# Modulated norms with plain transposes: the shift leaves the matmul and is added per feature tile when PSUM is emptied

## The chip, the cores and the metric

The kernel runs on one core of a Trainium2 chip, in one launch. The metric is the device time of one execution in microseconds (us), taken as the median of several executions; one execution of the kernel before was also recorded by the hardware profiler. Engines are named as in the profile: PE is the matrix engine (PEld its weight loads), DVE the vector engine, ACT the scalar engine, POOL the GpSimd engine, SP the engine that issues most of the DMAs. A name such as L598 is a line of the kernel.

## The reference

A stack of transformer blocks on 256 tokens of width 1024, batch 1, all in f32. The first two blocks use plain RMS norms; the last two ("mix2" and "ffn2", two layers each) are conditioned on a vector c: per layer a product of silu(c) with a matrix (1024 x 6144) gives six vectors of 1024, a shift, a scale and a gate for each half of the block.

```python
y = x * rsqrt(mean(x * x, axis=-1) + 1e-6)
h = y * (n * (1 + scale)) + shift      # per feature, before mix2 and before ffn2
x = x + gate * mix2(h)                 # three mixers side by side, one output product
x = x + gate * ffn2(h)                 # causal depthwise conv on a gated feed-forward
```

What matters here is the second line: a norm whose result has a per-feature shift added, and which must reach the products with features on the 128 partitions.

## The kernel before

The 256 tokens are two token tiles of 128 (t = 0, 1), the 1024 features eight feature tiles of 128 (k = 0 to 7). x is kept with tokens on partitions. Every large product is done in three passes: each operand is split into a rounded high part and the low remainder (h_hi and h_lo for activations, wh and wl for weights), and hi*hi, lo*hi and hi*lo are accumulated in PSUM. A weight tile is brought by a DMA on SP's queue into raw, rounded to wh by ACT (CAST, L464), and its remainder wl is made by POOL (L467) or DVE (L469).

The program runs eight stages one after the other; the last four are m0 (mix2, layer 0, from about 787 us), f2 (ffn2, layer 0, from 967), m1 (mix2, layer 1, from 1184) and f3 (ffn2, layer 1, from 1367, to the end at 1569). Each of the four begins with a norm with shift, and these four norms are all that the change touches. The other norms have no shift.

A norm (`_norm`, L582) works per token tile and per half of the features. DVE multiplies x by the inverse root and by `row`, a copy of n * (1 + scale) on all partitions (L595), which gives xn. A PSUM tile ps_t of 128 x 512 then takes four 128 x 128 blocks. Without a shift each is a PE transpose (L605). With a shift a first matmul (L598) writes the shift into all of ps_t: its operand is the last 128 columns of the tile `row`, which are zero (a POOL memset, L557) but for eight rows that hold the shift (a DMA, L558), and the other operand is the identity, broadcast. The four blocks are then added by ordinary matmuls with the identity (L603), into the same accumulation. Emptying is the same for both: one ACT copy of 128 x 512 rounds ps_t to h_hi (L608), one DVE subtraction of 128 x 512 makes h_lo (L609).

Who reads h: in m0 and m1 `rwkv_scores` computes ps_lk (eight feature tiles of three matmuls for t0, then the same for t1; L492, L493, L494 of `mm3_b`) and copies each result out (a_raw, L1527), and the other mixers follow on the same h. In f2 and f3 `first_units` (L612) computes ps_gt in the same way for each token tile, copies it (first_raw, L627) and transposes it (L634); all further units use ps_gu (L480, L483).

The conditioning vectors come from 24 products on DVE per layer (`ada_step`, L1394), each on a 1 MB piece that ACT's queue brings (L1378); those of layer 1 run during f2. `mod_rows` packs the results, transposes them on PE and writes them to DRAM, from where `load_row` (L551) fetches the rows back. The shift is in the 48-column tile mods[l] with features on partitions as well, columns 0 to 7 for the mixer and 24 to 31 for the feed-forward.

The order of the instructions on each engine is not written by hand: the kernel's framework schedules every engine's queue from the program order, priorities and its own time estimates. Each engine then runs its queue strictly in that order, so an instruction that waits holds up all that is behind it.

## Time and profile before

| | |
|---|---|
| median of 3 runs | 1570.32 us (1565.72 to 1572.02) |
| the profiled execution | 1570.74 us, span in the trace 1569.0 us |
| mean granted PE clock | 0.972 of full speed |
| PE busy | 1455.1 us (93% of the span) |
| PE weight loads | 1286.3 us (82%) |
| DVE busy | 1120.2 us (71%) |
| ACT busy | 811.7 us (52%) |
| POOL busy | 659.3 us (42%) |

How to read it: the share of an engine is an average over eight stages that have different limits, so the rows further down come from single stages. A timeline row gives the start, the time until the end of the group, the engine, the line, the operation with the tiles that it writes and reads, the count, and in brackets how long the engine had been idle and what released it. PE's matmuls overlap, so the distance between two starts tells what one costs, not its duration.

### The profile page before, as it was taken

The numbers are of one execution on the slowest core, as the hardware profiler recorded it, in microseconds if no ns is written. First come the engines' busy times: TensorE is split into PE (matmuls) and PEld (weight loads), VectorE is DVE, ScalarE is ACT, GpSimd is POOL, SyncE is SP. The second block draws the span as 40 slices with busy tenths as digits, with TensorE's granted clock in tenths as the row PEclk, the third lists the DMA queues.
The fourth block names the chain that finished last, engine by engine and source line by source line (L and its number), as shares of the span: only waits on it lengthen the run. The fifth ranks groups of instructions, "written<-read, shape, count | busy, mean of one in ns | idle before, by whom it ended". The sixth has DMA issues, their size and how long they took to land. (4 is left out here: it accounts for less than half of the span.)

```text
span 1569.0 us, 25783 instructions
## 1 busy us (share of the span) xinstructions
PE 1455.1 (93%) x9586; PEld 1286.3 (82%) x9586; DVE 1120.2 (71%) x2352; ACT 811.7 (52%) x1474; POOL 659.3 (42%) x433
## 2 busy tenths in 40 slices
PE   5999989899999899999988988998998899899998
PEld 4998878699988788999877766898987776589987
DVE  3588668778686577887477597788876768766752
ACT  4676545544543464554354665455544465466651
POOL 3577623256452522443136312465644622236530
PEclk9999999999999999999998999999999999999999
DMA  4756622677884455988434325576773442465551
GB/s 159 232 167 189 182 69 68 209 289 281 298 306 131 136 182 188 337 313 311 170 115 128 108 78 184 203 285 252 264 247 126 120 130 72 141 202 180 191 188 38
DMA packets 103246, 292.96 MB, mean 187 GB/s; under 512 B 28072, under 2 KB 37968, under 8 KB 96976
## 3 DMA queue, kind: packets, MB, share of 16 engines
q1 hardware_dynamic: 93872, 237.12, 44.9%
q10 hardware_dynamic: 8896, 53.14, 9.2%
q8 instruction: 75, 1.23, 0.3%
q0 software_dynamic: 352, 1.06, 0.2%
q14 instruction: 51, 0.42, 0.1%
HBM read 288.04 MB, written 3.24 MB: 186 GB/s over the span
## 5 line engine op out<-in xcount | busy, mean ns | idle before, releaser
L467 POOL TENSOR_TENSOR wl<-raw,wh 128x1024 fp32r<-128x1024 f32 (+4 forms) x162 | 405.6, 2511 | 414.6 <-ACT wh L464 350.7
L464 ACT CAST wh<-raw 128x1024 fp32r<-128x1024 f32 (+3 forms) x421 | 424.1, 1018 | 249.1 <-PE ps_o L493 97.4
L469 DVE TENSOR_TENSOR wl<-raw,wh 128x1024 fp32r<-128x1024 f32 (+2 forms) x259 | 356.9, 1385 | 145.2 <-ACT wh L464 143.2
L480 PE MATMUL ps_gu<-h_hi,wh 128*128 128x256 f32 x1280 | 313.1, 283 | 6.9 <-DVE gu_u L2226 6.3
L480 PE MATMUL ps_gu<-h_lo,wh 128*128 128x256 f32 x1280 | 312.7, 283 | 0.0
L480 PEld LDWEIGHTS ps_gu<-h_hi,wh 128*128 128x128 f32 x1280 | 244.9, 191 | 7.6 <-issue 6.7
L480 PEld LDWEIGHTS ps_gu<-h_lo,wh 128*128 128x128 f32 x1280 | 245.0, 191 | 0.1
L1394 DVE CUSTOM_DVE_ANT_0 ada_raw<-ada_raw,ada_cond 128x1024 f32<-128x1024 f32 x96 | 160.5, 1685 | 68.7 <-DMA ada_raw<-in_ada 68.7
L483 PE MATMUL ps_gu<-h_hi,wl 128*128 128x256 f32 x1280 | 179.2, 283 | 5.9 <-DVE wl L469 3.9
L483 PEld LDWEIGHTS ps_gu<-h_hi,wl 128*128 128x128 f32 x1280 | 164.4, 192 | 6.5 <-DVE wl L469 4.1
L494 PE MATMUL ps_o<-wl,act_h 128*128 128x512 f32 x352 | 138.8, 394 | 0.0
L493 PE MATMUL ps_o<-wh,act_l 128*128 128x512 f32 x352 | 138.6, 394 | 0.0
L492 PE MATMUL ps_o<-wh,act_h 128*128 128x512 f32 x352 | 138.3, 393 | 0.0
L2226 DVE SCALAR_TENSOR_TENSOR gu_u<-ps_gu,f2s,gu_u 128x254 f32<-128x254 f32 (+1 forms) x176 | 82.0, 477 | 40.7 <-ACT gu_u L2224 38.6
L738 POOL TENSOR_TENSOR act_l<-gu_t,act_h 128x256 fp32r<-128x256 f32 x44 | 51.8, 1179 | 102.7 <-ACT act_h L737 102.7
L2229 POOL TENSOR_TENSOR gu_t<-gu_t,gu_u 128x256 f32<-128x256 f32 x44 | 47.4, 1078 | 97.4 <-DVE gu_u L2226 84.1
L494 PEld LDWEIGHTS ps_o<-wl,act_h 128*128 128x128 f32 x352 | 66.1, 188 | 15.4 <-issue 0.5
L493 PEld LDWEIGHTS ps_o<-wh,act_l 128*128 128x128 f32 x352 | 66.1, 188 | 15.1 <-issue 0.2
L492 PEld LDWEIGHTS ps_o<-wh,act_h 128*128 128x128 f32 x352 | 66.1, 188 | 15.0 <-issue 0.2
L737 ACT CAST act_h<-gu_t 128x256 fp32r<-128x256 f32 x44 | 17.7, 407 | 95.8 <-DVE gu_t L736 95.8
L480 PE MATMUL ps_g<-h_hi,wh 128*128 128x256 f32 x256 | 66.5, 294 | 0.0
L480 PE MATMUL ps_g<-h_lo,wh 128*128 128x256 f32 x256 | 66.2, 293 | 0.0
(662 smaller groups left out, 2978.1 us busy)
## 6 DMA issues: line engine op xcount, KB each, us to landing
ada_raw<-in_ada ACTq DMA_DIRECT2D x48, 1024.0 KB, 6.2
raw<-in_f_gu SPq DMA_DIRECT2D x88, 512.0 KB, 5.4
raw<-in_u_gu SPq DMA_DIRECT2D x88, 512.0 KB, 4.2
raw<-in_f_dn SPq DMA_DIRECT2D x44, 512.0 KB, 6.2
raw<-in_u_dn SPq DMA_DIRECT2D x44, 512.0 KB, 4.3
raw<-in_g_qkv SPq DMA_DIRECT2D x32, 512.0 KB, 3.5
raw<-in_g_z SPq DMA_DIRECT2D x16, 512.0 KB, 5.7
raw<-in_g_out SPq DMA_DIRECT2D x16, 512.0 KB, 3.7
```

Of the source, the lines that this page charges most:

```text
L464: self.last_copy = nc.scalar.copy(wh[:, :cols], raw[:, :cols])
L467: nc.gpsimd.tensor_tensor(wl[:, :cols], raw[:, :cols], wh[:, :cols].bitcast(F32), op=ALU.subtract)
L469: nc.vector.tensor_tensor(wl[:, :cols], raw[:, :cols], wh[:, :cols].bitcast(F32), op=ALU.subtract)
L480: nc.tensor.matmul(ps, wh[:, k * width + m0 : k * width + m0 + m], xx[:, k, :], start=(n == 0), stop=(n == last))
L483: self.last_mm = nc.tensor.matmul(ps, wl[:, k * width + m0 : k * width + m0 + m], xh[:, k, :], start=False, stop=(n == last))
L492: nc.tensor.matmul(ps, xh, wh[:, sl], start=start, stop=False, **kw)
L493: nc.tensor.matmul(ps, xl, wh[:, sl], start=False, stop=False, **kw)
L494: nc.tensor.matmul(ps, xh, wl[:, sl], start=False, stop=stop, **kw)
L738: nc.gpsimd.tensor_tensor(al[:, m, :], t, ah[:, m, :].bitcast(F32), op=ALU.subtract)
L1394: nc.vector.tensor_tensor_reduce(raw[:, j], raw[:, j], self.cond, 1.0, 0.0, op0=ALU.mult, op1=ALU.add, accum_out=mod[:, i : i + 1])
L2226: nc.vector.scalar_tensor_tensor(u[:, j, d:], ps[:, j, : S - d], cw[:, 3 * q + 2 - d : 3 * q + 3 - d], u[:, j, d:], op0=ALU.mult, op1=ALU.add)
L2229: nc.gpsimd.tensor_tensor(t, t, u[:, 0], op=ALU.mult)
```

## The change

The shift matmul, the 128 extra columns of `row`, their memset and the DMA of the shift are gone. Norms with a shift now use the plain transposes. Emptying is per feature tile: ACT's activation (Identity, with the shift as a bias column) makes one 128 x 128 block of h_hi, and one DVE instruction, (ps_t + shift) - h_hi, makes the block of h_lo. `mod_rows` packs four vectors rather than six, which drops two small DVE copies per layer. `norm_steps` gets the columns of mods[l] in place of True.

```diff
-    def load_row(self, src, shift=None, queue=None):
-        self.row = self.xp.tile([128, D + 128], F32, name="row", tag="row")
-        queue = queue or self.nc.sync
-        queue.dma_start(self.row[:, :D], src.partition_broadcast(128))
-        if shift is not None:
-            self.nc.gpsimd.memset(self.row[:, D:], 0.0)
-            queue.dma_start(self.row[0:8, D:], shift)
+    def load_row(self, src, queue=None):
+        self.row = self.xp.tile([128, D], F32, name="row", tag="row")
+        (queue or self.nc.sync).dma_start(self.row, src.partition_broadcast(128))
...
                         ps = self.pm.tile([128, 4, 128], F32, name="ps_t", tag="mm")
-                        if shift:
-                            nc.tensor.matmul(ps, self.row[:, D:], self.ident[:, 4 * i : 4 * i + 4].unsqueeze(2).to_broadcast([128, 4, 128]), start=True, stop=False, skip_group_check=True)
                         for j in range(4):
                             k = i * 4 + j
-                            xk = xn[:, k * 128 : k * 128 + 128]
-                            if shift:
-                                nc.tensor.matmul(ps[:, j, :], xk, self.ident, start=False, stop=j == 3, skip_group_check=True)
-                            else:
-                                nc.tensor.transpose(ps[:, j, :], xk, self.ident)
+                            nc.tensor.transpose(ps[:, j, :], xn[:, k * 128 : k * 128 + 128], self.ident)
                         tk = slice(t * 128, t * 128 + 128)
+                        if shift is not None:
+                            for j in range(4):
+                                k = i * 4 + j
+                                nc.scalar.activation(h[:, k, tk], ps[:, j], AF.Identity, bias=shift[:, k : k + 1], scale=1.0)
+                                nc.vector.scalar_tensor_tensor(l[:, k, tk], ps[:, j], shift[:, k : k + 1], h[:, k, tk].bitcast(F32), op0=ALU.add, op1=ALU.subtract)
+                            continue
                         hs, ls = (a[:, 4 * i : 4 * i + 4, tk] for a in (h, l))
                         nc.scalar.copy(hs, ps)
                         nc.vector.tensor_tensor(ls, ps, hs.bitcast(F32), op=ALU.subtract)
...
-            self.load_row(self.next_mod[0], self.next_mod[4], nc.gpsimd)
+            self.load_row(self.next_mod[0], nc.gpsimd)
...
-            hl, norm = self.norm_steps(x, True, lambda t: xn[t])
+            hl, norm = self.norm_steps(x, self.mods[l][:, 0:8], lambda t: xn[t])
...
-        self.load_row(self.rows[1], self.rows[5])
+        self.load_row(self.rows[1])
...
-            hl, norm = self.norm_steps(x, True, lambda t: xn[t])
+            hl, norm = self.norm_steps(x, self.mods[l][:, 24:32], lambda t: xn[t])
```

The finer instructions also come out in another order on ACT, DVE and PE, in the four stages alone (in the changed code the lines are three to five lower). Three places matter.

ACT at the start of m1, from the first h_hi on (ps_t to h_hi is the emptying, CAST wh the rounding of a weight tile, a_raw the copy of a finished ps_lk). Before:

```order
L608 CAST h_hi<-ps_t 128x4x128
L565 ACTIVATE ps_o,ss<-x_t 128x512
L608 CAST h_hi<-ps_t 128x4x128
L1910 ACT_TABLE_LOAD
L1910 ACTIVATE b_ls<-b_ls 128x2
L1527 COPY a_raw<-ps_lk 128x388
L608 CAST h_hi<-ps_t 128x4x128 x2
L464 CAST wh<-raw 128x1024 x3
L1527 COPY a_raw<-ps_lk 128x388
```

After:

```order
L601 ACTIVATE h_hi<-ps_t,mod_7554 128x128 x2
L561 ACTIVATE ps_o,ss<-x_t 128x512
L601 ACTIVATE h_hi<-ps_t,mod_7554 128x128 x2
L1905 ACT_TABLE_LOAD
L1905 ACTIVATE b_ls<-b_ls 128x2
L601 ACTIVATE h_hi<-ps_t,mod_7554 128x128 x4
L1522 COPY a_raw<-ps_lk 128x388
L601 ACTIVATE h_hi<-ps_t,mod_7554 128x128 x5
L464 CAST wh<-raw 128x1024
L601 ACTIVATE h_hi<-ps_t,mod_7554 128x128 x3
L464 CAST wh<-raw 128x1024 x2
L1522 COPY a_raw<-ps_lk 128x388
```

The table load moved from behind the eighth feature tile of t0 to behind the fourth, and one CAST now stands between the fifth and the sixth of the eight pieces of t1 (those after the first a_raw); the first a_raw stayed between the two token tiles.

ACT at the start of f3. Before:

```order
L608 CAST h_hi<-ps_t 128x4x128 x2
L464 CAST wh<-raw 128x1024 x3
L627 COPY first_raw<-ps_gt 128x512
L464 CAST wh<-raw 128x1024
L608 CAST h_hi<-ps_t 128x4x128 x2
L464 CAST wh<-raw 128x1024 x5
```

After:

```order
L601 ACTIVATE h_hi<-ps_t,mod_7554 128x128 x3
L464 CAST wh<-raw 128x1024
L601 ACTIVATE h_hi<-ps_t,mod_7554 128x128 x4
L464 CAST wh<-raw 128x1024
L601 ACTIVATE h_hi<-ps_t,mod_7554 128x128 x2
L464 CAST wh<-raw 128x1024 x2
L601 ACTIVATE h_hi<-ps_t,mod_7554 128x128 x2
L464 CAST wh<-raw 128x1024
L601 ACTIVATE h_hi<-ps_t,mod_7554 128x128
L464 CAST wh<-raw 128x1024
L624 COPY first_raw<-ps_gt 128x512
```

All of t0's h_hi stood ahead of the first CAST; now its fourth to seventh feature tiles stand behind one CAST and its eighth behind two. The row of two after the second CAST holds the last tile of t0 and the first of t1, so four of t1's pieces now stand ahead of first_raw, where none did; three more follow it (not shown), and the last stands behind one more CAST.

DVE in f2, from the last multiplication of the norm on (ISA is the product of ada_step with its accumulator read). Before:

```order
L595 SCALAR_TENSOR_TENSOR xn<-x_t,rstd,row 128x512
L609 TENSOR_TENSOR h_lo<-ps_t,h_hi 128x4x128
L469 TENSOR_TENSOR wl<-raw,wh 128x1024 x3
L609 TENSOR_TENSOR h_lo<-ps_t,h_hi 128x4x128
L1394 ISA ada_raw,mod_7558<-ada_raw,ada_cond 128x1024
L1394 ISA mod_7558 128x1
```

After:

```order
L592 SCALAR_TENSOR_TENSOR xn<-x_t,rstd,row 128x512
L602 SCALAR_TENSOR_TENSOR h_lo<-ps_t,mod_3410,h_hi 128x128 x3
L469 TENSOR_TENSOR wl<-raw,wh 128x1024
L602 SCALAR_TENSOR_TENSOR h_lo<-ps_t,mod_3410,h_hi 128x128 x9
L1391 ISA ada_raw,mod_7554<-ada_raw,ada_cond 128x1024
L1391 ISA mod_7554 128x1
L1391 ISA ada_raw,mod_7554<-ada_raw,ada_cond 128x1024
L1391 ISA mod_7554 128x1
L602 SCALAR_TENSOR_TENSOR h_lo<-ps_t,mod_3410,h_hi 128x128
L469 TENSOR_TENSOR wl<-raw,wh 128x1024 x2
```

The last piece of h_lo moved from ahead of the first ada product to behind the first two.

## Rows read from the trace of the kernel before

**Rows 1.** Windows, m0 and f2: us, busy PE, PEld, DVE, ACT, POOL; clock.

```profile
786.00:968.00 182.00, 161.01 (x940) 127.51 (x938) 137.73 (x508) 103.04 (x228) 71.21 (x64) 0.97 0.36 113
968.00:1184.00 216.00, 200.69 (x1317) 183.13 (x1317) 171.61 (x235) 108.50 (x170) 104.10 (x67) 0.96 0.69 248
```

**Rows 2.** Tile ps_t by form: counts, ns min/median/max, first and last start.

```profile
L598 PE MATMUL ps_t<-ident,row x32: 590/592/595, 788.5 to 1365.9; 128*128 128x512 f32 x32
L603 PE MATMUL ps_t<-ident,xn x128: 270/275/422, 794.0 to 1376.8; 128*128 128x128 f32 x128
L605 PE MATMUL ps_t<-ident,xn x48: 272/273/474, 303.5 to 606.7; 128*128 128x128 f32 x48
L608 ACT CAST h_hi<-ps_t x32: 558/586/598, 12.4 to 1378.7; 128x512 fp32r<-128x512 f32 x32
L609 DVE TENSOR_TENSOR h_lo<-ps_t,h_hi x32: 675/686/693, 18.3 to 1380.9; 128x512 fp32r<-128x512 f32 x32
```

**Rows 3.** Timeline of PE, t1 of m1.

```profile
1192.25 1.02 PE L598 MATMUL ps_t<-ident,row 128*128 128x512 f32 x2
1193.11 1.05 PE L603 MATMUL ps_t<-ident,xn 128*128 128x128 f32 x8
1194.00 1.03 PE L598 MATMUL ps_t<-ident,row 128*128 128x512 f32 x2
```

**Rows 4.** Timeline of PE at the starts of f2, f3 and m0.

```profile
962.99 3.60 PE L598 MATMUL ps_t<-ident,row 128*128 128x512 f32 x8
967.95 2.05 PE L603 MATMUL ps_t<-ident,xn 128*128 128x128 f32 x16 [1.36 <-DVE xn L595]
1367.15 2.05 PE L603 MATMUL ps_t<-ident,xn 128*128 128x128 f32 x16 [0.64 <-DVE xn L595]
793.97 2.05 PE L603 MATMUL ps_t<-ident,xn 128*128 128x128 f32 x16 [2.48 <-DVE xn L595]
```

**Rows 5.** Lines by form, small PSUM reads: total us, mean ns, idle before.

```profile
L2136 ACT CAST d_yh<-ps_do 128x128 fp32r<-128x128 f32 x8 | 2.2, 272 | 1.4 <-PE ps_do L2135 1.4
L1009 ACT ACTIVATE ps_kq<-ps_kq,rk 128x128 f32<-128x128 f32 x16 | 5.5, 346 | 2.0 <-PE ps_kq L1006 1.8
L2137 DVE TENSOR_TENSOR d_yl<-ps_do,d_yh 128x128 fp32r<-128x128 f32 x8 | 2.3, 288 | 7.3 <-ACT d_yh L2136 7.2
```

**Rows 6.** Timeline of ACT, t1 of m0.

```profile
803.25 1.28 ACT L1910 ACT_TABLE_LOAD   x1
805.34 3.18 ACT L464 CAST wh<-raw 128x1024 fp32r<-128x1024 f32 x3
```

**Rows 7.** Timelines of ACT, PE and DVE in f2.

```profile
971.38 1.04 ACT L464 CAST wh<-raw 128x1024 fp32r<-128x1024 f32 x1 [5.56 <-DMA raw<-in_u_gu]
986.77 0.39 PE L492 MATMUL ps_gt<-wh,h_hi 128*128 128x512 f32 x1
987.46 0.60 PE L634 MATMUL ps_gu<-ident,first_raw 128*128 128x128 f32 x4
988.34 1.23 DVE L1394 CUSTOM_DVE_ANT_0 ada_raw<-ada_raw,ada_cond 128x1024 f32<-128x1024 f32 x1 [4.90 <-DMA ada_raw<-in_ada]
```

**Rows 8.** Timelines of ACT and PE in f3.

```profile
1374.68 2.23 ACT L464 CAST wh<-raw 128x1024 fp32r<-128x1024 f32 x2 [2.87 <-DMA raw<-in_u_gu]
1381.08 0.80 PE L493 MATMUL ps_gt<-wh,h_lo 128*128 128x512 f32 x1 [1.59 <-DVE h_lo L609]
1382.10 0.63 PE L492 MATMUL ps_gt<-wh,h_hi 128*128 128x512 f32 x1
1386.37 0.58 PE L493 MATMUL ps_gt<-wh,h_lo 128*128 128x512 f32 x1
```

**Rows 9.** Windows of PE in f1 and f3: us, busy, clock, DMA share, GB/s.

```profile
604.00:606.00 2.00, 0.34 (x3) 1.00 0.77 256
1381.00:1383.00 2.00, 1.92 (x5) 0.50 0.98 293
```

**Rows 10.** Waits of PE in m0: total us, times, longest.

```profile
PE ps_qk L1947 <- DVE b_ro L1943: 3.6, 1, 3.6
```

More of the change, by code (lines that the diff above doesn't have):

```diff
@@ L568, in stats, with norm_t @@
         self.rstd[t] = rstd
-    def norm_t(self, x, shift=False):
+    def norm_t(self, x, shift=None):
         hl, steps = self.norm_steps(x, shift)
@@ L574, in norm_t, with norm_steps @@
         return hl
-    def norm_steps(self, x, shift=False, xns=None):
+    def norm_steps(self, x, shift=None, xns=None):
         h = self.hp.tile([128, KD, S], F32R, name="h_hi", tag="h", bufs=2)
@@ L1403, in mod_rows @@
         mod = self.mods[l]
-        c = pool.tile([128, 6, 8], F32, name="mod_c")
+        c = pool.tile([128, 4, 8], F32, name="mod_c")
         mv = mod.rearrange("p (i k) -> p i k", i=6)
@@ L1408, in mod_rows @@
             nc.vector.tensor_copy(c[:, 2 + i], mv[:, 3 * i + 2])
-            nc.vector.tensor_copy(c[:, 4 + i], mv[:, 3 * i])
-        ps = self.pm.tile([48, 128], F32, name="ps_mr", tag="mm")
+        ps = self.pm.tile([32, 128], F32, name="ps_mr", tag="mm")
         nc.tensor.transpose(ps, c.rearrange("p i k -> p (i k)"), self.ident)
-        t = pool.tile([48, 128], F32, name="mod_t")
+        t = pool.tile([32, 128], F32, name="mod_t")
         nc.scalar.copy(t, ps)
-        d = self.dr.tile([48, 128], F32, name=f"mod_d{l}")
+        d = self.dr.tile([32, 128], F32, name=f"mod_d{l}")
         nc.scalar.dma_start(d, t)
-        rows = [d[8 * i : 8 * i + 8] for i in range(6)]
-        self.next_mod = [r.rearrange("a b -> (a b)") for r in rows[:4]] + rows[4:]
+        self.next_mod = [d[8 * i : 8 * i + 8].rearrange("a b -> (a b)") for i in range(4)]
     def gate_row(self, i, pool):
```

## The prediction

> **What bounds the kernel now.** I read the shares first, then the busy time by stage, then the timelines of the four places where a norm with shift stands. PE is busy for 1455.1 of 1569.0 us, so time taken off PE looks like time taken off the kernel. The stages are to be read apart, though. f2 is bound by PE (200.7 of 216 us), m0 less so (161.0 of 182), with DVE at 137.7 and ACT at 103.0 [rows 1]: in the mixers PE waits at times for a chain through DVE and ACT, for instance once for 3.6 us before ps_qk [rows 10]. At the start of a stage PE waits for xn, then for the first h_hi and h_lo, and what counts is the delay until each feature tile of h can be used.
>
> **What leaves PE.** A shift matmul is two instructions. In t1 of m1 the pair starts at 1192.25 and the blocks behind it at 1193.11: 0.86 us. The eight instructions for four blocks take until 1194.00, 0.89 us, 0.11 each [rows 3]. A plain transpose lasts as long as one of those (273 against 275 ns) but is one instruction where the matmul with the identity is two: 48 rows for 48 blocks against 128 for 64 [rows 2]. So 16 pairs x 0.86 = 13.8 us and 64 instructions x 0.11 = 7.0 us go, 20.8 us of PE in all.
>
> Not all of it is on the path. In f2 the four pairs run in 962.99 to 966.59, and PE then still waits 1.36 us for xn; f3 has its four pairs in the same place and waits 0.64 us, and m0 runs its first two before a wait of 2.48 us [rows 4]. These ten pairs, 8.6 us, buy nothing: the wait for xn grows by as much. On the path are the two pairs of t1 in m0 and all four of m1, of which the first two stand among the last output matmuls that xn waits for: 6 x 0.86 = 5.2 us. The blocks save 16 x 0.11 = 1.8 us in each stage. Gross, m0 gains 1.7 + 1.8 = 3.5, m1 3.4 + 1.8 = 5.2, f2 1.8 and f3 1.8, together 12.3 us.
>
> **What is added on ACT and DVE.** 16 emptyings of 0.586 us on ACT and 0.686 on DVE [rows 2] become 64 pieces on each. The trace has no Identity with a bias on 128 x 128; the nearest rows that read PSUM are a CAST of that size at 0.272 and an activation with a scale column at 0.346, and on DVE a subtraction at 0.288 [rows 5]. For ACT I take 0.30 (instructions overlap a little at their ends), so a group of four is 1.2 against 0.59, 16 x 0.6 = 9.6 us more; the ends are 16 x 0.5 = 8 and 16 x 0.8 = 12.8. For DVE I take 0.30 as well, 16 x 0.5 = 8 us; the ends are 0.288 and the whole row's 0.686, a fourth of the width not costing more than all of it. Neither is near its limit on average, so this is priced where PE waits. The first piece is there about 0.3 us sooner than the first whole group; a feature tile keeps PE busy for 0.69 us (986.77 to 987.46, three matmuls [rows 7]), so pieces at 0.30 stay ahead where nothing stands between them.
>
> The Trainium skill (Perfetto Trace Analysis, Optimizing Scalar/DVE Operations) speaks against such splitting: each instruction pays a fixed access cost, given as about 51 ns for ScalarE and 125 ns for DVE on PSUM, and larger operations are advised. By those figures, as an estimate, the split would add 16 x 3 x 0.051 = 2.4 us on ACT and 16 x 3 x 0.125 = 6.0 us on DVE, where the rows give 8 to 13 and about 8. The same section grants that smaller pieces let another engine start sooner.
>
> **What gives time back: the queues.** The finer pieces are scheduled between weight roundings, and each engine keeps its order.
>
> m0: ACT rather than PE sets the second a_raw, with which ps_lk is handed on. The table load (1.28) and three CASTs (3.18, until 808.52) stood ahead of it [rows 6], and still do: the new order there is a_raw, three pieces, table load, two pieces, CAST, two pieces, CAST, one piece, CAST, a_raw. The pieces of t1 take 8 x 0.3 = 2.4 us in place of 2 x 0.59. ACT may begin sooner, but its queue is 1.2 longer, so little of the 3.5 passes: -0.3, with ends at -3.5 and +1.2.
>
> m1: here one CAST stands among t1's pieces, which hides behind PE's work, and two of 1.0 before the second a_raw (2.0); one more CAST stands ahead of what follows (1.0); the earlier start is cut by about 0.9, since xn has its own DVE chain. -5.2 + 3.9 = -1.3, with ends at -5.2 and +1.2 (only the longer queue is left).
>
> f2: the one piece ahead of the CAST that waits for data until 971.38 [rows 7] lets PE start one feature tile (0.69) earlier; that is within the 1.8. The last piece of h_lo now stands behind two ada products. Their data landed at 988.34, when ps_gt of t1 was already over (987.46), and a product takes 1.2 us [rows 7]. The ada transfers stand 1 to 2 us sooner in ACT's queue, so I put the last piece at 989.3. PE would need it for the second matmul of the last tile, 0.46 before 987.46, less 1.8: at 985.2. Seven ps_gu matmuls of half the width (half of 0.23 each) now stand ahead of that one on PE and cover 0.8. The wait is 3.3, less 1.8 gained: +1.5, with ends at -1.8 (no wait) and +5 (B below).
>
> f3: t0's last tile stands behind two CASTs, the second of which waited for data until 1374.68 [rows 8], so t0 ends 1.5 to 2.5 us later. In return t1's pieces no longer all wait for first_raw and another CAST. PE waited 1.59 us for h_lo at 1381.08, and its clock was at 0.50, the lower of its two levels (1.2 GHz), in the products behind: 1382.10 to 1386.37 is ten steps of 0.43 instead of 0.23 [rows 8, 9], 2 us lost. I expect the wait to be cut to a third and the lower clock to be shorter: -1.8 - 1.0 - 1.6 + 1.9 = -2.5. The ends are -6.3 (all of wait, clock and blocks gained and no delay) and +2.9 (the delay of t0 stays and nothing comes back).
>
> The two small copies per layer, the memset and the small DMA go from engines with room and are costed at nothing: the copies lie among the ada products, the memset on POOL behind its wait for ps_t. If POOL's weight remainders were late, they would come sooner; that is no loss.
>
> Sum: -0.3 - 1.3 + 1.5 - 2.5 = -2.6 us against the profiled 1570.74, which lies 0.4 above the median: 1568.1 on its scale, 1567.7 on the median's. The mixers behind the norms come out in another order on all three engines; I cannot price that, and bound it by one wait like that of 3.6 us [rows 10] more or less in each mixer. A difference of 0.5% (7.85 us) is about what a measurement here can tell from none.
>
> **Rivals.**
>
> A, faster: the gross gain of 12.3 us arrives, since the pieces keep ahead of PE and the mixers start earlier: 1570.3 - 12.3 = 1558.0. For it speaks PE's share of 93%. Against it speak ACT's and DVE's new orders.
>
> B, slower: pieces stand behind work that waits for data. It decides at two places. If the ada data lands as late as before, f2's last h_lo comes at 988.34 + 2.4 + 0.3 = 991.0, which is 991.0 - 985.2 - 0.8 - 1.8 = +3.2; with one more transfer or product waited for it is +5, and I take 4. f3's end of the range adds 2.9, and a CAST of about 1.0 in each mixer that falls ahead of what PE waits for another 2.0; the unpriced order of the mixers is not in it. 1570.3 + 8.9 = 1579.2. The point is f2's last h_lo after 990.5 together with f3's t0 ending after 1378. For it speak the rows of waits for data at both places [rows 7, 8].
>
> C, the clock: the matmuls that go ran in gaps and kept PE active, and transposes take the place of matmuls. If each of the four starts then had one stretch at the lower level as f3 had (2 us), that is some 6 us over the forecast, f3 having its own already: 1573.7. The trace speaks against it: in f1, whose norm has plain transposes and no shift, a stretch with PE busy 0.34 of 2 us kept a clock of 1.00 [rows 9]. The Trainium skill (TensorE: Matmul & The Clock Gate, Part 4: PE-mode transpose) says that transpose mode does not count as busy for the gate in the same way; by that rule C would be the forecast, at 1573.7, and f1 does not bear it out.
>
> **How the numbers follow.** Forecast 0.45, A 0.27, B 0.20, C 0.08. The predicted time is the forecast's, 1567.7. Its own range is 1562 to 1574, from f3's two ends and the mixers. The whole range, 1556 to 1581, takes in A and B with 2 us on the far side of each. Faster by over 0.5% (under 1562.5) is A with a small part of the forecast, 0.30; slower (over 1578.2) is most of B and a fringe of the forecast and of C in which the mixers' order turns out badly, 0.23; the rest, 0.47, is no change.
>
> **What would show it.** L598 is gone from PE, and its busy time falls by some 20 us, while the span falls by a seventh of that. ps_t's pieces last 0.27 to 0.35 on ACT and about 0.3 on DVE. PE waits for xn at the starts of f2 and f3 for about 5 and 4 us instead of 1.36 and 0.64. In f2 one ps_gt matmul of t1 waits some 3 us for h_lo behind the ada products. In f3 ps_gt of t0 ends near 1377 less what the stages ahead gain, with no single wait of over 1 us in t1. The forecast is wrong if m1's second a_raw comes over 3 us earlier and the mixers keep it (A), if f2's wait for h_lo is over 5 us (B), or if the granted clock falls to 0.50 in the mixers' first products (C).

## The result, and the profile after

The changed kernel is slower: 1582.51 us in the median (1581.48 to 1584.65, 4 runs) against 1568.02 for the kernel before (1564.40 to 1572.02, 4 runs, run beside it). The ratio is 1.0106, 95% interval 1.0077 to 1.0135. The forecast was no change at 1567.7, range 1556 to 1581, so the time lies outside the range and on the side to which I gave 0.23.

The profiled execution took 1581.48 us. Its span and busy times:

```profile
span 1579.8 us, 25669 instructions
PE 1448.7 (92%) x9490; PEld 1281.0 (81%) x9490; DVE 1138.7 (72%) x2396; ACT 822.5 (52%) x1522; POOL 658.5 (42%) x427
```

PE has 96 matmuls less than before, as counted in the forecast (32 of the shift pairs, 64 of the blocks), but only 6.4 us less busy time: the same matmuls took longer, since the mean granted clock is 0.964 instead of 0.972. DVE gained 18.5 us and ACT 10.8. The tile ps_t, instructions by form (counts, shortest, median and longest duration in ns, first and last start), answers to [rows 2]:

```profile
L596 PE MATMUL ps_t<-ident,xn x112: 270/273/476, 301.9 to 1390.2; 128*128 128x128 f32 x112
L601 ACT ACTIVATE h_hi<-ps_t,mod x64: 350/367/387, 791.6 to 1397.9; 128x128 fp32r<-128x128 f32 x64
L602 DVE SCALAR_TENSOR_TENSOR h_lo<-ps_t,mod,h_hi x64: 334/345/974, 792.3 to 1399.1; 128x128 fp32r<-128x128 f32 x64
```

A plain transpose lasts 273 ns, as expected; a piece takes 367 ns on ACT and 345 on DVE.

To see where the time went, I cut the last 790 us at marks that every kernel has. "Start" is from the first block of xn on PE (a transpose, or a matmul with the identity) to the last a_raw (m0, m1) or to the last ps_gt (f2, f3); "rest" is from there to the first block of the next stage's norm, or to the last output matmul. Each is a difference of two starts in the timelines (us). The second line is a second trace of the kernel before, taken later (a run below), and shows how far such a number moves by itself.

| kernel | m0 start | m0 rest | f2 start | f2 rest | m1 start | m1 rest | f3 start | f3 rest |
|---|---|---|---|---|---|---|---|---|
| before | 14.7 | 159.3 | 19.3 | 197.3 | 15.7 | 166.9 | 21.7 | 175.4 |
| before, again | 14.7 | 160.0 | 18.3 | 194.3 | 15.7 | 167.2 | 18.9 | 175.4 |
| changed | 19.1 | 167.8 | 20.5 | 191.4 | 18.7 | 171.4 | 20.3 | 174.9 |

The two mixers together became 20 us longer, 13 of them in m0: 4.4 us in its norm and 8 us behind it, where nothing was changed but the order. m1 is longer by 3 and 4 us in the same two places; the 4 us are less sure than they look (see "Where the loss sits"). f2 and f3 lose little or nothing. The mark from which m0's start counts came 3.4 us earlier in the changed kernel, of which nothing is left at the end; it moves by 3 us between traces of the kernel before and of variants that are the same up to it (790.8 to 794.0).

The windows of m0, before and then after, cut at the second a_raw (length, then busy time of PE, PEld, DVE, ACT, POOL, the granted clock, DMA share, GB/s):

```profile
794.00:809.00 15.00, 14.72 (x89) 13.40 (x89) 11.55 (x42) 8.50 (x13) 2.26 (x3) 1.00 0.49 155
809.00:968.00 159.00, 140.78 (x832) 110.60 (x830) 119.39 (x445) 91.08 (x207) 66.00 (x59) 0.97 0.36 111
```

```profile
790.00:808.00 18.00, 14.39 (x63) 12.10 (x64) 13.75 (x54) 10.23 (x24) 1.99 (x2) 0.81 0.44 145
808.00:977.00 169.00, 144.21 (x829) 114.88 (x827) 123.44 (x441) 92.72 (x210) 66.95 (x59) 0.93 0.32 101
```

Behind the norm, 829 matmuls kept PE busy for 144.2 us where 832 took 140.8, at a clock of 0.93 instead of 0.97, and DVE was busy 4 us longer. In the norm the clock is 0.81 instead of 1.00.

The timeline of ACT for token tile 1 of m0 in the changed kernel (start, length, operation, count, idle time before and what ended it; one row of 0.2 us behind the table load is left out) shows what became of two whole emptyings of 0.59 us:

```profile
799.67 0.37 ACT L601 ACTIVATE h_hi<-ps_t,mod 128x128 fp32r<-128x128 f32 x1 [1.26 <-PE ps_t L596]
800.46 0.37 ACT L601 ACTIVATE h_hi<-ps_t,mod 128x128 fp32r<-128x128 f32 x1 [0.42 <-DVE h_lo L602]
801.01 0.37 ACT L601 ACTIVATE h_hi<-ps_t,mod 128x128 fp32r<-128x128 f32 x1 [0.19 <-PE ps_t L596]
801.40 1.28 ACT L1905 ACT_TABLE_LOAD   x1
802.80 0.61 ACT L601 ACTIVATE h_hi<-ps_t,mod 128x128 fp32r<-128x128 f32 x2
803.30 1.04 ACT L464 CAST wh<-raw 128x1024 fp32r<-128x1024 f32 x1
804.24 0.64 ACT L601 ACTIVATE h_hi<-ps_t,mod 128x128 fp32r<-128x128 f32 x2
806.96 1.04 ACT L464 CAST wh<-raw 128x1024 fp32r<-128x1024 f32 x1 [2.09 <-POOL c_w L2143]
807.91 0.36 ACT L601 ACTIVATE h_hi<-ps_t,mod 128x128 fp32r<-128x128 f32 x1
```

The second piece starts 0.79 us after the first: it waited 0.42 us for DVE's h_lo, although it needs nothing that DVE makes. Into the gaps the schedule put the table load and two CASTs, one of which waited 2.1 us for POOL, and the eighth piece starts 8.2 us after the first.

The other waits of the forecast are in the timelines of PE (f2, then f3) and of DVE (f2):

```profile
977.57 0.66 PE L596 MATMUL ps_t<-ident,xn 128*128 128x128 f32 x4 [3.71 <-DVE xn L592]
997.77 0.49 PE L493 MATMUL ps_gt<-wh,h_lo 128*128 128x512 f32 x1 [1.31 <-DVE h_lo L602]
1379.63 1.97 PE L596 MATMUL ps_t<-ident,xn 128*128 128x128 f32 x8 [4.12 <-DVE xn L592]
995.07 1.23 DVE L1391 CUSTOM_DVE_ANT_0 ada_raw<-ada_raw,ada_cond 128x1024 f32<-128x1024 f32 x1 [2.58 <-DMA ada_raw<-in_ada]
997.37 0.35 DVE L602 SCALAR_TENSOR_TENSOR h_lo<-ps_t,mod,h_hi 128x128 fp32r<-128x128 f32 x1
```

PE waits 3.7 and 4.1 us for xn where it waited 1.36 and 0.64 [rows 4]: the shift matmuls had indeed filled a wait. The last h_lo of f2 does stand behind two ada products, but their data landed early enough that PE waited 1.31 us for it, not 3.3.

### The profile page after: what moved, and what is told of

Its sections match the earlier page's. It is cut to its first block, busy times and chain, and to the rows that moved or that the text cites. A ratio compares the mean times of both kernels' runs of the same rounds, so it can differ in the third digit from the quotient of the medians.

```text
span 1579.8 us, 25669 instructions
## 1 busy us (share of the span) xinstructions
PE 1448.7 (92%) x9490; PEld 1281.0 (81%) x9490; DVE 1138.7 (72%) x2396; ACT 822.5 (52%) x1522; POOL 658.5 (42%) x427
## 4 chain that ended last, share of the span: by engine, by line
PE 57%; DVE 14%; ACT 4%; issue 3%; DMA 3%; POOL 2%; SPq 0%; ACTq 0%; POOLq 0%; DVEq 0%
PE ps_gu L480 15%; PE ps_gu L483 7%; PE ps_o L492 7%; PE ps_o L493 7%; PE ps_o L494 7%; DVE wl L469 3%; ACT wh L464 1%; DVE gu_u L2221 1%; DVE ada_raw L1391 1%; DMA ada_raw<-in_ada 1%; DMA raw<-in_u_gu 1%; DVE rs_t L519 1%; PE ps_u L480 1%; POOL wl L467 1%; DVE xn L592 1%
## 5 line engine op out<-in xcount | busy, mean ns | idle before, releaser
L1391 DVE CUSTOM_DVE_ANT_0 ada_raw<-ada_raw,ada_cond 128x1024 f32<-128x1024 f32 x96 | 166.5, 1748 | 63.4 <-DMA ada_raw<-in_ada 56.3
L493 PEld LDWEIGHTS ps_o<-wh,act_l 128*128 128x128 f32 x352 | 66.2, 188 | 14.6
L492 PEld LDWEIGHTS ps_o<-wh,act_h 128*128 128x128 f32 x352 | 66.2, 188 | 14.6
```

The source lines that it names most:

```text
L492: nc.tensor.matmul(ps, xh, wh[:, sl], start=start, stop=False, **kw)
L493: nc.tensor.matmul(ps, xl, wh[:, sl], start=False, stop=False, **kw)
L1391: nc.vector.tensor_tensor_reduce(raw[:, j], raw[:, j], self.cond, 1.0, 0.0, op0=ALU.mult, op1=ALU.add, accum_out=mod[:, i : i + 1])
```

## The experiments

Each but one (the kernel before itself) was timed in several rounds against the kernel before on the same chip; a ratio is given with its 95% interval. Four theories ran through them. S: the pieces of one PSUM tile make ACT and DVE take turns. C: the missing matmuls lower PE's clock, and that costs the time. Q: there are simply more small instructions on ACT and DVE. O, added after the first four runs: the new order of the mixers behind the norm costs the time.

### Grouping the pieces

```diff
                             for j in range(4):
                                 k = i * 4 + j
                                 nc.scalar.activation(h[:, k, tk], ps[:, j], AF.Identity, bias=shift[:, k : k + 1], scale=1.0)
+                            for j in range(4):
+                                k = i * 4 + j
                                 nc.vector.scalar_tensor_tensor(l[:, k, tk], ps[:, j], shift[:, k : k + 1], h[:, k, tk].bitcast(F32), op0=ALU.add, op1=ALU.subtract)
```

> The changed kernel, with the four ACT pieces of a PSUM tile written ahead of its four DVE pieces instead of alternating with them. Theory S (sharing a bank): the pieces of one ps_t wait for each other across ACT and DVE, tile by tile, which stretches the norms and lets work be scheduled between them; grouped, ps_lk of t1 in the first mixer should end some 4 us sooner after the first transposes than in the changed kernel (15 us as before instead of 19), and the whole falls by 8 us or more, to 1574 or less. Theory C (clock): what counts is that the shift matmuls and the ordinary matmuls are gone, which grouping doesn't bring back: 1580 or more, and the clock still falls to 0.50 at the starts of the mixers. Theory Q (queues of ACT and DVE filled by more instructions): there are as many instructions as in the changed kernel, so within 4 us of it.

Measured: 1563.64 us, ratio 0.9983 (0.9968 to 0.9997). The two loops instead of one take back all of the loss and are 0.17% faster than the kernel before. Q falls: the instructions are the same in number and kind. C as the cause falls too: the clock over m0's start is as low as in the changed kernel (0.81). ACT in m0 (the eight pieces of t0, then four and four of t1, around the table load):

```profile
789.62 2.18 ACT L601 ACTIVATE h_hi<-ps_t,mod 128x128 fp32r<-128x128 f32 x8 [0.35 <-PE ps_t L596]
798.06 1.14 ACT L601 ACTIVATE h_hi<-ps_t,mod 128x128 fp32r<-128x128 f32 x4 [0.42 <-PE ps_t L596]
800.62 1.13 ACT L601 ACTIVATE h_hi<-ps_t,mod 128x128 fp32r<-128x128 f32 x4
```

Eight pieces in 2.2 us, 0.26 apart, where the changed kernel took 0.4 to 0.8 for each. m0's start is 16.0 us, f2's 17.9, m1's 16.9, f3's 17.6: 10 us less than in the changed kernel over the four. Of the 4.4 us that m0's start had lost, 3.1 come back, of m1's 3.0 it is 1.8. m0's rest is 164.3. The edit changes the order behind the norms as well: by the traces, PE's order in m1 is again that of the kernel before, and in m0 it is a third one. So this run alone does not part S from the order.

### Plain transposes, emptied whole

```diff
-                        if shift is not None:
-                            for j in range(4):
...
-                            continue
```

> The changed kernel with plain transposes, emptied whole as the norms without shift are (one ACT copy and one DVE subtraction of 128 x 512); the shift is left out of the sum. It is the PE half of the change alone. S and Q: the on-path part of the PE saving arrives, 5 to 12 us below the kernel before, 1556 to 1563. C: the clock falls at the starts of the norms as in the changed kernel, and the time is no better than the kernel before, 1568 to 1580.

Measured: 1571.79 us, ratio 1.0042 (1.0024 to 1.0060), for a kernel that leaves the shift out. The time lies in C's range, not in that of S and Q, and the clock is low at three of the four starts, though not at m1's. But the four starts are the shortest of the first four experiments (14.6, 17.6, 12.8, 18.1), so the PE saving and the whole emptying do what they should there. What is lost is lost behind them: m0's rest took 170.6 us, 11 more than before. This was the first sign that a gain in the norm can be lost behind it, which none of S, C and Q says.

### Filling PE's place again

```diff
+                        if shift is not None:
+                            nc.tensor.matmul(ps, self.row[:, 0:128], self.ident[:, 4 * i : 4 * i + 4].unsqueeze(2).to_broadcast([128, 4, 128]), start=True, stop=True)
                         for j in range(4):
```

> The changed kernel with a matmul of the old shift matmul's shape ahead of each four transposes, whose result the transposes overwrite; 13.8 us of PE work come back in the same places. C: the starts of the mixers keep the full clock as before, and the time falls by 5 us or more although PE has more to do. S and Q: the pairs that lie on the path are paid again, 0 to 8 us above the changed kernel, 1582 to 1590.

Measured: 1585.82 us, ratio 1.0124 (1.0094 to 1.0153), as S and Q had it. The windows of PE at m0's start (length, busy, granted clock, DMA share, GB/s), of the changed kernel and of this one:

```profile
790.00:794.00 4.00, 3.40 (x13) 0.60 0.17 20
```

```profile
788.00:792.00 4.00, 3.45 (x18) 1.00 0.36 99
```

The clock is back at 1.00, so the missing matmuls do lower it. (With the filler PE also waits less for xn there, 1.57 us instead of 3.28.) But m0's start is as long as in the changed kernel (19.3 us): a PE that waits for pieces gains nothing from a full clock. C's mechanism is there and is not the cause. m0's rest is 164.9 us, 3 less than in the changed kernel, but m1's is 175.8, 4 more: what comes behind a norm moves by several us from one version to the next.

### Pieces under the old matmuls

```diff
+                        if shift:
+                            for j in range(4):
+                                k = i * 4 + j
+                                nc.scalar.copy(h[:, k, tk], ps[:, j])
+                                nc.vector.tensor_tensor(l[:, k, tk], ps[:, j], h[:, k, tk].bitcast(F32), op=ALU.subtract)
+                            continue
                         hs, ls = (a[:, 4 * i : 4 * i + 4, tk] for a in (h, l))
```

> The kernel before, shift matmul and all, emptied in 128 x 128 pieces (ACT copy, DVE subtraction, alternating) in the four norms with shift. It is the emptying half of the change alone. S: slower than the kernel before by 8 us or more. Q: the pieces without a bias are shorter (0.27 and 0.29 us), so slower by 3 to 8 us. C: no matmul is gone, so within 4 us of the kernel before.

Measured: 1575.53 us, ratio 1.0058 (1.0039 to 1.0077), 9 us: the alternating pieces, with the order that they cause, do about half of the harm. In m0 the order behind the second a_raw is that of the changed kernel, and the rest is 168.6 us. That led to theory O.

### The kernel before, once more

> The kernel before once more, for a second trace. All theories: within 5 us of its median. If the rest of m0 (from the second a_raw to the first transposes of f2) again takes about 159 us where every kernel with new pieces or transposes took 164 to 171, that difference belongs to the order of the mixers and not to chance; f2 after its start took 197 us before and 191 to 195 in the others, and if that is chance it falls to about 192 here.

Measured: 1564.35 us. m0's rest is 160.0, m1's 167.2, so these repeat. f2's rest is 194.3: the 197.3 of the first trace was partly chance, and differences of 3 us there (and in the starts of f2 and f3, 18.3 and 18.9 here) say nothing.

### Where the loss sits

The change in f2 and f3 alone, the matmul shift and the whole emptying again in m0 and m1 (True selects the old norm, as in the kernel before):

```diff
-            hl, norm = self.norm_steps(x, self.mods[l][:, 0:8], lambda t: xn[t])
+            hl, norm = self.norm_steps(x, True, lambda t: xn[t])
```

> The change in f2 and f3 alone (plain transposes, alternating pieces with the shift); m0 and m1 keep the shift matmul and whole emptying, and the mixers their order. S: the alternation costs some 1 to 3 us at each of the two starts, and the rest of the loss is in the mixers: 0 to 5 us above the kernel before, 1565 to 1570. O (the new order of the mixers is the loss): the same or better, 1560 to 1566. If the loss of the changed kernel sat in f2 and f3: 1575 or more.

Measured: 1566.21 us, ratio 1.0004 (0.9986 to 1.0022): no loss, inside S's range and 0.2 us above O's. The changed kernel with m0's norm put back:

```diff
-            hl, norm = self.norm_steps(x, self.mods[l][:, 0:8], lambda t: xn[t])
+            hl, norm = self.norm_steps(x, self.mods[l][:, 0:8] if l else True, lambda t: xn[t])
```

> The changed kernel with m0's norm alone put back (shift matmul, matmuls with the identity, whole emptying); PE's order in m0 is then word for word that of the kernel before, in m1 that of the changed kernel, in f2 and f3 within 90 rows of it. O and S together: m0 gives back its 4.4 us at the start and 8 to 9 us behind it, the rest of the change stays: 12 to 13 us below the changed kernel, 1568 to 1572. If the cost were spread evenly over the four norms: a quarter back, 1577 to 1580.

Measured: 1574.30 us, ratio 1.0050 (1.0029 to 1.0071). m0 is as before (14.7 and 159.4), but the total fell by 8 us, not by 12 to 13, between the two forecasts: the median moved less than m0 did, since m1's rest was 175.7 here against 171.4. By the three ratios, m0 makes 0.0106 - 0.0050 = 0.0056 of the loss, about 9 us, m1 0.0050 - 0.0004 = 0.0046, about 7 us, and f2 and f3 nothing (times 1565; each is uncertain by 4 to 6 us).

m1's rest is a weak witness. By the traces, the order of PE, ACT and POOL there is that of the kernel before in ten of the fourteen traces of this document, where the rest is 166.9 to 171.5 us, and that of the changed kernel in four, where it is 170.7 to 175.8. On average that is 4 us, but the two ranges overlap, and the 171.4 of the changed kernel lies in both.

### A bank for each piece

In f2 and f3 each block gets a PSUM tile of its own; the pieces still alternate.

```diff
...
+                            for j in range(4):
+                                k = i * 4 + j
+                                pj = self.pm.tile([128, 128], F32, name="ps_t", tag="mm")
+                                nc.tensor.transpose(pj, xn[:, k * 128 : k * 128 + 128], self.ident)
+                                nc.scalar.activation(h[:, k, tk], pj, AF.Identity, bias=shift[:, k : k + 1], scale=1.0)
+                                nc.vector.scalar_tensor_tensor(l[:, k, tk], pj, shift[:, k : k + 1], h[:, k, tk].bitcast(F32), op0=ALU.add, op1=ALU.subtract)
+                            continue
```

> The changed kernel, pieces still alternating ACT, DVE, but in f2 and f3 each 128 x 128 block has a PSUM tile, and so a bank, of its own; m0 and m1 as in the changed kernel. S (sharing a bank makes ACT and DVE take turns): in f2 and f3 the pieces of ACT follow each other without waiting for DVE, and the time from the first transposes to the end of ps_gt falls from 20.5 and 20.3 us to about 18 each; 3 to 6 us below the changed kernel, 1577 to 1580. If it is the alternating program order as such and not the bank: no change at those two places, 1582.

Measured: 1582.27 us, ratio 1.0113 (1.0084 to 1.0143), no better than the changed kernel as a whole. The emptying rows of ACT at the start of f2, for token tile 0, in the changed kernel (the first six of its eight pieces) and then here:

```profile
978.26 0.37 ACT L601 ACTIVATE h_hi<-ps_t,mod 128x128 fp32r<-128x128 f32 x1 [2.03 <-PE ps_t L596]
981.66 0.62 ACT L601 ACTIVATE h_hi<-ps_t,mod 128x128 fp32r<-128x128 f32 x2
982.44 0.63 ACT L601 ACTIVATE h_hi<-ps_t,mod 128x128 fp32r<-128x128 f32 x2 [0.16 <-DVE h_lo L602]
984.62 0.37 ACT L601 ACTIVATE h_hi<-ps_t,mod 128x128 fp32r<-128x128 f32 x1 [1.54 <-PE ps_t L596]
```

```profile
975.64 1.14 ACT L599 ACTIVATE h_hi<-ps_t,mod 128x128 fp32r<-128x128 f32 x4 [1.70 <-PE ps_t L598]
978.81 1.14 ACT L599 ACTIVATE h_hi<-ps_t,mod 128x128 fp32r<-128x128 f32 x4
```

With a tile for each block, ACT runs four pieces in 1.14 us without a wait for DVE, as S says; written in the same alternation, they now come out grouped. So the turns come from the shared tile. f2's start fell from 20.5 to 16.7 us, as expected, but not by the turns alone: in the changed kernel a CAST that waited 2.08 us for its data stood behind the first piece, here it stands behind the fourth. f3's start did not fall (22.0 after 20.3); the clock there was at 0.50 for 11.8 us instead of 5.1. And f2's rest was 5 us longer (196.2), so nothing is left of the gain. The Trainium skill (PSUM — Partial Sum Buffer, PSUM bank collisions raise a hardware error) says that two engines must not touch one bank on the same partitions at the same time, two readers included, and that software has to put a dependency between them; the wait of ACT for DVE on a shared tile, 0.42 us above, and its absence here agree. What the chip does without such a wait was not tried.

### Only the order

These two put O to the test. Both are the kernel before with its matmuls, in which h of token tile 1 alone, in m0 and m1, is emptied in pieces of copy and subtraction; one alternates them, the other groups them. They have the same instructions. Alternating:

```diff
+                        if self.plan.get("order") and shift and t == 1:
+                            for j in range(4):
+                                k = i * 4 + j
+                                nc.scalar.copy(h[:, k, tk], ps[:, j])
+                                nc.vector.tensor_tensor(l[:, k, tk], ps[:, j], h[:, k, tk].bitcast(F32), op=ALU.subtract)
+                            continue
```

(The plan entry "order" is that of the mixers, m0 and m1.)

> The kernel before, with matmuls and all, where only h of token tile 1 in m0 and m1 is emptied in alternating 128 x 128 pieces (copy on ACT, subtraction on DVE, no bias). In m0 this makes the framework give PE the order of the changed kernel (two rows apart) behind the norm; in m1, f2 and f3 PE's order stays that of the kernel before. O (the order of m0 behind the norm costs): the stretch from the second a_raw of m0 to the first transposes of f2 takes 167 to 170 us instead of 159 to 161, and the whole is slower by 6 to 10 us, 1572 to 1577. S alone: only the norm of t1 is stretched, 1 to 4 us, 1567 to 1571, and the stretch behind it stays at 159 to 161.

Grouped, as against the one above:

```diff
-                                k = i * 4 + j
-                                nc.scalar.copy(h[:, k, tk], ps[:, j])
-                                nc.vector.tensor_tensor(l[:, k, tk], ps[:, j], h[:, k, tk].bitcast(F32), op=ALU.subtract)
+                                nc.scalar.copy(h[:, i * 4 + j, tk], ps[:, j])
+                            for j in range(4):
+                                nc.vector.tensor_tensor(l[:, i * 4 + j, tk], ps[:, j], h[:, i * 4 + j, tk].bitcast(F32), op=ALU.subtract)
```

> The same pieces in the same token tiles as in the run before this, the same instructions in number and kind, but written four of ACT and then four of DVE. The order on PE, ACT and DVE outside the norm is word for word that of the kernel before. O: the stretch in m0 takes 159 to 161 us and the whole is within 3 us of the kernel before. Were it the number of small instructions: as slow as the run before this.

Measured: alternating 1576.85 us, ratio 1.0075 (1.0050 to 1.0101); grouped 1567.16, ratio 1.0017 (0.9996 to 1.0037). Both came out in O's ranges. m0's norm itself differs by 2.2 us (16.9 against 14.7), m0's rest by 9.8: 169.4 against 159.6.

The alternating kernel holds a control of its own. In m1 token tile 1 is emptied in turns too, but the order behind it stays that of the kernel before:

```profile
1201.57 0.27 ACT L610 CAST h_hi<-ps_t 128x128 fp32r<-128x128 f32 x1 [0.36 <-DVE h_lo L611]
1202.20 0.27 ACT L610 CAST h_hi<-ps_t 128x128 fp32r<-128x128 f32 x1 [0.36 <-DVE h_lo L611]
```

There nothing is lost: m1's start is 15.7 us as before, its rest 167.9 (166.9 and 167.2 before). Turns without a new order cost nothing there; in m0, with one, they cost 12 us. Over all fourteen traces, m0's rest is 167.8 to 169.4 us in the four that have the changed kernel's order there and 159.1 to 161.4 in the seven that have the old one; the other three have orders of their own.

Windows of the rest, grouped and then alternating (columns as above for m0):

```profile
808.00:966.00 158.00, 138.55 (x825) 109.11 (x823) 118.35 (x443) 90.65 (x206) 66.30 (x59) 0.98 0.37 110
```

```profile
808.00:977.00 169.00, 147.36 (x824) 115.66 (x822) 125.29 (x442) 91.11 (x207) 64.82 (x59) 0.92 0.33 100
```

The same matmuls (825 and 824 of them are in the windows) kept PE busy for 138.6 and 147.4 us, at 0.98 and 0.92, while its idle time, 19.5 and 21.6 us, differs by 2 us only. Most of the 10 us is PE at a lower clock: in the whole rest it ran at 0.50 for 6.8 us in the grouped kernel, in two stretches, and for 27.3 in the alternating one, in five. What starts it can be read some 6 us behind the norm. In the grouped kernel DVE finishes a_k of token tile 1 and then scales a_P, and PE waits 2.12 us for a_sq:

```profile
812.28 0.47 DVE L1506 SCALAR_TENSOR_TENSOR a_k<-ps_k,lay,a_k 128x255 f32<-128x255 f32 x1
813.16 0.29 DVE L1549 TENSOR_SCALAR a_P<-a_P 64x256 f32<-64x256 f32 x1
812.89 0.39 PE L1560 MATMUL ps_ks<-small,a_sq 128*128 128x4 f32 x2 [2.12 <-ACT a_sq L1557]
```

In the alternating one ACT has a CAST ahead of its part in a_P and a_k, so POOL's weight remainder starts at 812.98, and DVE scales a_P ahead of a_k (POOL, two rows of DVE, PE):

```profile
812.98 2.39 POOL L467 TENSOR_TENSOR wl<-raw,wh 128x1024 fp32r<-128x1024 f32 x1
813.25 2.27 DVE L1549 TENSOR_SCALAR a_P<-a_P 64x256 f32<-64x256 f32 x1
815.55 0.48 DVE L1506 SCALAR_TENSOR_TENSOR a_k<-ps_k,lay,a_k 128x255 f32<-128x255 f32 x1
815.58 1.22 PE L1579 MATMUL ps_lr<-a_P,a_lora 128*128 128x256 f32 x2 [3.63 <-DVE a_P L1549]
```

The same 64 x 256 operation takes 2.27 us instead of 0.29 while POOL runs. It ends at 815.52, 0.15 us after POOL's subtraction (812.98 + 2.39 = 815.37). Counted from the second a_raw, a_k is 2.3 us later on DVE; PE waits 3.63 us for a_P where it waited 2.12 for a_sq, and the clock falls in that wait and stays down behind it. PE some 7 us behind the second a_raw, grouped and then alternating (length, busy, clock, DMA share, GB/s):

```profile
814.00:824.00 10.00, 9.20 (x72) 1.00 0.16 41
```

```profile
814.00:824.00 10.00, 8.43 (x31) 0.50 0.13 40
```

In the same 10 us PE does 72 matmuls in the one and 31 in the other. All four kernels in which m0 has this order (changed, own banks, pieces under old matmuls, this one) have an a_P of 2.27 us there; all seven traces with m0's old order have 0.29. It is not the only place for such a loss: with plain transposes emptied whole, a_P took 0.60 us, m0's rest was as long, 170.6, and the operation ahead of a_P was the one held up, 1.95 us where the alternating kernel has 0.35 for the same form, again ending 0.15 us after POOL:

```profile
810.97 1.95 DVE L1539 TENSOR_SCALAR a_kkn<-a_k,lay 128x256 f32<-128x256 f32 x1
810.36 2.41 POOL L467 TENSOR_TENSOR wl<-raw,wh 128x1024 fp32r<-128x1024 f32 x1
```

That the order is the cause in m0 is shown by the pair and by m1 beside it, the first loss by the rows. The alternating kernel's lag, at equal matmuls, grows from 3.3 us at the last ps_ks over 6.2 us (some 75 us behind the second a_raw) to 10.9 at the last ps_o; what sets off each of the later stretches at 0.50 I have not taken apart.

### A version faster than both

Grouped pieces with plain transposes in f2 and f3 only, m0 and m1 as before, so that the mixers keep their order:

> f2 and f3 with plain transposes and grouped pieces (four of ACT, then four of DVE); m0 and m1 as in the kernel before. O: with the mixers in their old order and the f stages' starts at 18 us (grouped) instead of 19.3 and 21.7, 4 to 9 us below the kernel before, 1556 to 1561. S alone: like the grouped kernel of all four norms, 1562 to 1566. C: the clock falls at the starts of f2 and f3 and gives it back, 1564 to 1569.

Measured: 1567.84 us, ratio 1.0002 (0.9984 to 1.0020): C's line came true, not O's. The edit is the two loops of the first experiment together with the one line above that puts m0 and m1 back. The same with one filler matmul ahead of each half of t0 in f2 and f3, in the wait for xn:

```diff
+                            if t == 0:
+                                nc.tensor.matmul(ps, self.row[:, 0:128], self.ident[:, 4 * i : 4 * i + 4].unsqueeze(2).to_broadcast([128, 4, 128]), start=True, stop=True)
```

> The kernel with grouped pieces in f2 and f3 alone (m0 and m1 as before), and with a matmul of the old shift matmul's shape ahead of each four transposes of t0 in f2 and f3, overwritten by the transposes: it lies in the wait for xn. C: the clock stays at 1.00 at the starts of f2 and f3, the time from the first transposes to the end of ps_gt falls from 19.1 and 18.5 us to about 16, and the whole to 3 to 6 us under the kernel with grouped pieces in f2 and f3: 1561 to 1565. If the clock's fall there is not due to the missing matmuls: within 2 us of it, 1566 to 1569.

Measured: 1561.07 us, ratio 0.9977 (0.9963 to 0.9992): faster than the kernel before by 0.23%. Against the kernel with all four norms grouped (0.9983) it is not shown to be faster: 0.06% lies inside either interval. f2's and f3's starts are 15.9 and 16.6 us, against 19.1 and 18.5 without the filler. PE at the start of f2 (length, busy, clock, DMA share, GB/s), without and with the filler:

```profile
966.00:970.00 4.00, 1.97 (x8) 0.70 0.79 264
970.00:974.00 4.00, 2.67 (x8) 0.50 0.94 344
```

```profile
962.00:966.00 4.00, 2.22 (x9) 0.74 0.91 253
966.00:970.00 4.00, 3.66 (x15) 0.84 0.83 325
```

The clock does not stay at 1.00, as I had expected, but it is back sooner: 0.84 instead of 0.50 in the second window. By the ratios, matmuls that did no useful work bought 0.25% (0.9977 against 1.0002), hardly more than the uncertainty of the two (0.0015 and 0.0018). The two traces confirm only part of it: the starts of f2 and f3 are 5.1 us shorter and f2's rest is 2.9 us longer, while 5.6 of the 8.8 us by which the traced spans differ lie in m0 and m1, where the two kernels are the same.

The rule of the Trainium skill that the forecast named (TensorE: Matmul & The Clock Gate, Part 4: PE-mode transpose: transposes do not count as busy for the gate in the same way) would lower the clock at these places, and at m0's start above. That it is the transposes is not shown, since the filler also shortens the idle time ahead of them. With plain transposes emptied whole, PE waited only 1.44 us for xn at m1's start, and the clock stayed at 1.00:

```profile
1190.00:1194.00 4.00, 2.92 (x16) 1.00 0.71 229
```

At the same kernel's other three starts PE had waited 3.3 to 4.1 us, and the clock was 0.50 in the first 4 us.

## Why the prediction was wrong

1. **What leaves PE** was right in count (96 instructions), and so was the share that buys nothing: the waits for xn grew to 3.7 and 4.1 us. PE's busy time fell by 6.4 us, not by some 20, since the clock fell too.

2. **The pieces** cost 367 ns on ACT, above the upper end of 346 that I took, and 345 on DVE, within the ends. That is small: grouped, ACT starts one every 0.26 us. The step that failed is the sentence "pieces at 0.30 stay ahead where nothing stands between them". It priced each engine's pieces alone. On one PSUM tile they take turns, 0.4 to 0.8 us for a feature tile, and the schedule fills the gaps with other work. It also took the time that PE needs for a feature tile, 0.69 us, from f2; in the mixers, whose products are 388 wide instead of 512, it is 0.52 (the kernel before, two feature tiles in m0):

```profile
796.99 0.33 PE L492 MATMUL ps_lk<-wh,h_hi 128*128 128x388 f32 x1
797.51 0.34 PE L492 MATMUL ps_lk<-wh,h_hi 128*128 128x388 f32 x1
```

 I had the emptying of one tile by two engines in front of me as a pair, whole against whole, and did not ask what four pairs do. m0's start was forecast at -0.3 and came at +4.4, m1's at -1.3 and came at +3.0. Grouping takes back 3.1 and 1.8 of these; with alternating pieces under the old matmuls the two starts lose 2.2 and 0.3. So the turns are the larger part of it, not all, and in m0 one CAST's wait of 2.09 us for POOL, between the seventh and the eighth piece, is part of it too.

3. **The order of the mixers** is the larger error: "bound it by one wait like that of 3.6 us". Measured, it is 8 to 10 us in m0; in m1 it may be 4, but there the spread among kernels with the same order is as large. The bound took one wait, and an order changes many; and it took waits alone, where most of the cost is PE at a lower clock behind them (in the pair, 2 us more idle time and 9 us more busy time). That the order changes was known before; that it was worth a term of its own, larger than all the others, was not seen.

4. **f2 and f3**, on which the forecast spent most words, net to nothing (1.0004 with the change in them alone), within its ends. (Its ends for f3 do not follow from its own terms: blocks, wait and clock give -1.8 - 1.6 - 2.0 = -5.4, not -6.3, and the delay of t0 at most +2.5, not +2.9. Nothing here hangs on that.)

5. **Rival B** had the kind right, pieces behind other work and slower, at 1579.2; its places, f2's ada products and f3's CASTs, were wrong (PE waited 1.31 us where it put up to 5). **Rival C** had it right that the missing matmuls lower the clock, as the filler shows (0.60 against 1.00 at m0's start); that the transposes do is not shown, and its price was wrong: grouped, the kernel has these low stretches too and is still faster than before. **Rival A**'s 12.3 us came in no version; the fastest gained 0.23%, 3.6 us.

## What to carry to other kernels

Where two engines empty one PSUM tile piece by piece, write all pieces of the one ahead of all pieces of the other: the alternation, with the order that it caused, cost 1.2% here, and one split loop takes it back. A tile for each piece ends the turns too, but tried in two of the four norms it bought nothing as a whole (1.0113). In a kernel whose queues a scheduler orders, a change in one place must be priced with the order that it causes behind it; a control with the same instructions and the old order, such as the grouped pieces here, tells the two apart at the cost of one run.

## What the runs showed of the hardware

A DVE operation that took 0.29 us with POOL's weight subtraction still to come took 2.27 us beside it, in four kernels alike; that POOL holds it up is read from the rows and was not tried by itself. The Trainium skill (SBUF — State Buffer, SBUF: two separate sides) says that DVE and GpSimd share a pair of ports, and that where a DVE instruction uses it, the one of the two that starts first holds it for its whole instruction while the other is blocked. In the rows above POOL starts first both times, and the DVE operation ends 0.15 us after it, which agrees.

And PE can pay for a wait twice: in m0 of the alternating kernel nearly the same matmuls kept it busy 9 us longer, at 0.92 instead of 0.98, with only 2 us more idle time. Matmuls whose result is thrown away, put into the waits of f2 and f3, went with a faster kernel (0.9977 against 1.0002).
